# Softmax times V on one core: small tiles behind the large buffers, a flat spare loop, and loop code aligned to a fetch block

## The chip, the cores and the metric

The kernel runs on one core of a Trainium2 chip. The metric is the device time of one execution in microseconds; for a kernel's time the median of several executions is taken.

## The reference

```python
def reference(scores, v):          # scores [8, 12, 1024, 1024], v [8, 12, 1024, 64], float32
    scores_max = np.max(scores, axis=-1, keepdims=True)
    attn = np.exp(scores - scores_max)
    attn = attn / (np.sum(attn, axis=-1, keepdims=True) + 1e-8)
    return np.matmul(attn, v).astype(np.float32)
```

That is a softmax over the last axis of 96 given score matrices, each multiplied with its 1024 x 64 block of `v`. The scores are 403 MB, `v` and the output 25 MB each.

## The kernel before, in words

The 96 pairs of batch and head are called heads here. The main loop (`For_i` at L434) takes four heads an iteration (`AHEAD`), so it runs 24 times. It is of the kind "reg_based": the engines are not stopped between iterations, and semaphores only count upwards.

For each head, `heads` does the following. The scores of the head, 4 MB, have been loaded into one of four buffers `s_nat` (L218), with eight rows of the matrix in each of the 128 partitions. ScalarE takes `exp` of two rows per partition at a time without subtracting the maximum and writes float16 to `p_nat` (L386). TensorE transposes 128 x 128 blocks of that into PSUM (`psT`, L399); VectorE copies them to SBUF (`pt`, L406); TensorE multiplies them with `vones` (L165), which holds the head's `v` in float16 and a column of ones, so that the sum of each row comes out as column 64. VectorE takes the reciprocals of the sums into `seen` (L144) and scales the product into `out_sb` (L150). GpSimd copies the next `v` from `v_sb` into `vones` (L239). All loads and stores are issued by SyncE on one queue: `load_next` and `last` put the load of the head four further on behind the last use of the buffer, and the last iterations split the loads and stores into smaller ones.

Since the maximum is not subtracted and float16 is used, the kernel checks that this was allowed. `seen` collects the smallest and the largest reciprocal over the whole run, `v_seen` the range of `v` (L257). At the end of each iteration `judge` makes of these a count of partitions in which all was within bounds (`part`, `fits`, `right`, all tiles of 128 x 1 made by `small`) and leaves it in `count` (L274 to L298). Behind the loop every engine loads `count` into a register (L439) and compares it (L440):

```python
    good = nc.values_load(count[:], min_val=0, max_val=P)
    with tc.If(good < P, preferred_fallthrough_block=False):
        general()
```

`general()` is a plain float32 version with the maximum subtracted. With the data used here it is never run: each engine executes a few instructions of the other arm, jumps over the code of `general()` and goes on behind it to the closing barriers. In that arm SyncE, ScalarE, VectorE and TensorE bring the semaphores that `general()` would have raised to the values that they would have had.

`general()` has two nested loops: over the heads (one load of the scores, eight of `v`, one store) and inside it over the eight rows of a partition. The tiles `seen`, `v_seen`, `count` and those of `small` come from `const_pool`, which lies in SBUF ahead of `sb_pool` with the large buffers `s_nat`, `v_sb`, `p_nat`, `pt` and `out_sb`.

## Time and profile before

| | |
|---|---|
| median of three executions | 1073.61 us (1073.51 to 1074.58) |
| the profiled execution, its own time | 1074.27 us |
| its span, from the first to the last instruction | 1072.4 us |
| TensorE, weight loads, VectorE, ScalarE, GpSimd busy | 728.2, 694.7, 776.4, 740.4, 244.9 us |
| read from HBM, written | 436.21 MB, 25.17 MB |
| chain of work that ended last | DMA 60%, TensorE 10%, weight loads 6%, ScalarE 6%, VectorE 5% |

Busy times are summed over the span, so that none of the engines is busy for more than 72% of it. The DMA row of the 40 slices and the table of DMA queues count the 16 DMA engines of the core together. Names that end in q (SPq, DVEq) stand for the instructions that an engine's sequencer executes itself: branches, register moves, semaphores, DMA issues; the page does not count them as busy time. L12 is line 12 of the kernel.

### The profile page before, as it was taken

To read this page: it belongs to the slowest core of one execution; us is meant where nothing else is said; L and a number is where in the kernel's file an instruction comes from. 1 tells how busy PE (TensorE), PEld (TensorE's weight loads), DVE (VectorE), ACT (ScalarE), POOL (GpSimd) and SP (SyncE) were. 2 spreads that over 40 slices of the span, in tenths; PEclk is the share of its full clock that TensorE was granted. 3 is DMA by queue.
4 is the path that set the end of the run, shared out by engine and by line. 5 is a ranking of instruction groups with operands and counts; after the bars stand their busy time and mean duration, and the time that the engine had idled before them with its cause. 6 is when DMAs were issued, how large, how long until landed. Compare 5 with 4: busy or idle time off the path is not lost.

```text
span 1072.4 us, 33178 instructions
## 1 busy us (share of the span) xinstructions
PE 728.2 (68%) x12312; PEld 694.7 (65%) x12312; DVE 776.4 (72%) x1663; ACT 740.4 (69%) x480; POOL 244.9 (23%) x406
## 2 busy tenths in 40 slices
PE   2766766766766668676666766667767667667685
PEld 2665766666766667676666766666766667666574
DVE  1876776877767777777686776767767778677686
ACT  3766776766858667676666676766857667686684
POOL 3113112131121211221113112131121211222113
PEclk9887878878888788878887878878787788877888
DMA  9999999999999999999999999999999999999993
GB/s 395 433 417 431 428 439 431 430 425 438 433 433 431 429 433 423 438 430 430 430 429 432 430 433 431 430 431 432 426 441 431 433 430 429 432 423 438 430 423 139
DMA packets 25336, 453.09 MB, mean 423 GB/s; under 512 B 2800, under 2 KB 3312, under 8 KB 9712
## 3 DMA queue, kind: packets, MB, share of 16 engines
q1 hardware_dynamic: 25328, 453.00, 98.6%
q8 instruction: 4, 0.07, 0.0%
q14 instruction: 4, 0.03, 0.0%
HBM read 436.21 MB, written 25.17 MB: 430 GB/s over the span
## 4 chain that ended last, share of the span: by engine, by line
DMA 60%; PE 10%; PEld 6%; issue 6%; ACT 6%; DVE 5%; POOL 3%; SPq 1%; POOLq 1%; DVEq 0%; ACTq 0%; PEldq 0%
DMA s_nat<-in_scores_dram 60%; PE psT L399 6%; ACT p_nat L386 6%; PE psO L165 4%; PEld L399 4%; POOL vones L239 3%; PEld L165 2%; DVE pt L406 2%; DVE v_seen L257 1%; SPq L230 1%; SPq L218 0%; POOLq L239 0%; DVE v_seen L251 0%; DVE part L270 0%; POOLq L360 0%
## 5 line engine op out<-in xcount | busy, mean ns | idle before, releaser
L386 ACT ACTIVATE p_nat<-s_nat 128x2048 f16<-128x2048 f32 (+1 forms) x456 | 709.7, 1631 | 223.2 <-DMA s_nat<-in_scores_dram 176.6
L399 PE MATMUL psT<-order,p_nat 128*128 128x128 f16 x6144 | 571.0, 251 | 240.9 <-ACT p_nat L386 228.5
L406 DVE COPY pt<-psT 128x1024 f16<-128x1024 f16 x768 | 520.7, 687 | 221.8 <-PE psO L165 87.2
L399 PEld LDWEIGHTS <-p_nat 128*128 128x128 f16 x6144 | 462.1, 125 | 259.3 <-ACT p_nat L386 246.2
L239 POOL CAST vones<-v_sb 32x512 f16<-32x512 f32 x400 | 244.2, 610 | 819.3 <-PE L399 506.7
L165 PE MATMUL psO<-vones,pt 128*128 128x65 f16 x6144 | 360.0, 205 | 32.8 <-DVE v_seen L251 15.4
L165 PEld LDWEIGHTS <-pt 128*128 128x128 f16 x6144 | 301.9, 106 | 44.7 <-DVE pt L406 30.2
L150 DVE TENSOR_TENSOR out_sb<-psO,seen 64x256 f32<-64x256 f32 x384 | 161.9, 422 | 53.7 <-DMA out_dram<-out_sb 43.1
L386 ACT ACT_TABLE_LOAD x24 | 30.8, 1283 | 94.7 <-PE psO L165 49.9
L257 DVE TENSOR_REDUCE v_seen<-vones 128x1 f32<-128x512 f16 x96 | 65.6, 684 | 2.2
L294 PE MATMUL psO<-vones,right 128*1 128x1 f16 x24 | 3.9, 164 | 62.7 <-DVE right L278 62.7
L294 PEld LDWEIGHTS <-right 128*1 128x1 f16 x24 | 1.9, 79 | 65.7 <-DVE right L278 65.7
L144 DVE RECIPROCAL seen<-psO 128x4 f32<-128x4 f32 x192 | 33.8, 176 | 0.9 <-PE psO L165 0.2
L298 DVE CAST count<-psO 1x1 int32<-1x1 f32 x24 | 3.5, 146 | 6.1 <-PE psO L294 6.1
L274 DVE SCALAR_TENSOR_TENSOR part<-seen,fits 128x1 f32<-128x1 f32 x24 | 7.0, 291 | 0.8
L251 DVE TENSOR_REDUCE seen<-seen 128x1 f32<-128x33 f32 x24 | 4.5, 188 | 0.8
L278 DVE SCALAR_TENSOR_TENSOR right<-seen,part 128x1 f16<-128x1 f32 x24 | 4.2, 175 | 0.8
L252 DVE TENSOR_REDUCE seen<-seen 128x1 f32<-128x33 f32 x24 | 4.2, 176 | 0.0
L278 DVE SCALAR_TENSOR_TENSOR fits<-v_seen,part 128x1 f32<-128x1 f32 x24 | 3.6, 150 | 0.0
L252 DVE TENSOR_REDUCE v_seen<-v_seen 128x1 f32<-128x5 f32 x24 | 3.6, 148 | 0.0
L251 DVE TENSOR_REDUCE v_seen<-v_seen 128x1 f32<-128x5 f32 x24 | 3.5, 148 | 0.0
L270 DVE TENSOR_SCALAR part<-v_seen 128x1 f32<-128x1 f32 x24 | 3.5, 144 | 0.0
(10 smaller groups left out, 1.4 us busy)
## 6 DMA issues: line engine op xcount, KB each, us to landing
s_nat<-in_scores_dram SPq DMA_DIRECT2D x96, 4096.0 KB, 31.5
v_sb<-in_v_dram SPq DMA_DIRECT2D x24, 1024.0 KB, 18.8
out_dram<-out_sb SPq DMA_DIRECT2D x47, 512.0 KB, 26.3
s_nat<-in_scores_dram SPq DMA_DIRECT2D x2, 2048.0 KB, 32.3
s_nat<-in_scores_dram SPq DMA_DIRECT2D x1, 1536.0 KB, 32.6
s_nat<-in_scores_dram SPq DMA_DIRECT2D x3, 512.0 KB, 21.1
s_nat<-in_scores_dram SPq DMA_DIRECT2D x1, 1024.0 KB, 24.9
out_dram<-out_sb SPq DMA_DIRECT2D x1, 256.0 KB, 2.6
```

The source lines that it names most:

```text
L144: inverse = nc.vector.reciprocal(out=recip, in_=psO[:, :, D : D + 1])
L150: nc.vector.tensor_tensor(out=st["out_sb"][h * W : (h + 1) * W, t, b * G : (b + 1) * G, :], in0=psO[part, :, 0:D], in1=recip[part].to_broa ...
L165: product = nc.tensor.matmul(out=bank[:, g * M : (g + 1) * M], lhsT=pt[:, c * P : (c + 1) * P], rhs=st["vones"][:, c, 0:M], start=(c == 0) ...
L230: nc.sync.dma_start(out=v_sb[:].rearrange("x h s l d -> x (h s l d)"), in_=rows[bass.ds(n // AHEAD, 1)].rearrange("o x y -> (o x) y"),)
L239: spread = nc.gpsimd.tensor_copy(out=vones_bufs[k][s * Q : (s + 1) * Q, :, 0:D].rearrange("i (h l) d -> i h l d", l=L), in_=v_sb[k * Q : ( ...
L251: nc.vector.tensor_reduce(out=tile[:, 0:1], in_=tile[:, 0 : n + 1], axis=X, op=ALU.min)
L252: nc.vector.tensor_reduce(out=tile[:, n + 1 : n + 2], in_=tile[:, 1 : n + 2], axis=X, op=ALU.max)
L257: watch = nc.vector.tensor_reduce(out=v_seen[:, 1 + k : 2 + k], in_=vones_bufs[k][:, :, 0:D], axis=mybir.AxisListType.XY, op=ALU.max, appl ...
L278: nc.vector.scalar_tensor_tensor(out=out, in0=tile[:, 0:1], scalar=low, in1=part, op0=ALU.is_ge, op1=ALU.mult)
L386: exp = nc.scalar.activation(out=p_nat[:, g : g + rows, :].rearrange("p r (x v) -> p x r v", v=Q * L), in_=s_bufs[k][:, r + g : r + g + ro ...
L399: turned = nc.tensor.transpose(out=psT[:, c * P : (c + 1) * P], in_=p_row[:, c // L, c % L, :], identity=order16[:],)
L406: copy = nc.vector.tensor_copy(out=pt[:], in_=psT[:])
```

## The change

1. `seen`, `v_seen`, `count` and the tiles of `small` come from a new pool, `small_pool`, opened behind the large buffers. The large buffers thereby start at lower addresses, directly behind `vones`.
2. `general()` has one loop over 96 x 8 blocks of 128 rows in place of two nested ones, with three DMAs (one block of scores, the head's `v`, one block of the output), and uses `s_nat0` alone for its buffers.
3. The main loop names VectorE and SyncE in `head_align_engines`. For these two engines the loader puts the first instruction of an iteration at the start of a block of the size in which instructions are fetched; the padding in front of it is jumped over.

```diff
+    small_pool = ctx.enter_context(tc.tile_pool(name="small", bufs=1))
-    seen = const_pool.tile([P, 1 + AHEAD * R + 1], FP32, name="seen")
+    seen = small_pool.tile([P, 1 + AHEAD * R + 1], FP32, name="seen")
     nc.vector.memset(seen, 1.0)
-    v_seen = const_pool.tile([P, 1 + AHEAD + 1], FP32, name="v_seen")
+    v_seen = small_pool.tile([P, 1 + AHEAD + 1], FP32, name="v_seen")
     nc.vector.memset(v_seen, 1.0)
...
-        return const_pool.tile([P, 1], dtype, name=f"{name}{turn[name]}")
+        return small_pool.tile([P, 1], dtype, name=f"{name}{turn[name]}")
-    count = const_pool.tile([1, 1], I32, name="count")
+    count = small_pool.tile([1, 1], I32, name="count")
...
     def general():
-        s, x = s_bufs[0], s_bufs[1]
...
-        with tc.For_i(0, BH, 1) as n:
-            nc.sync.dma_start(out=s[:], in_=one(sc_bh, n))
-            for c in range(C):
-                nc.sync.dma_start(
-                    out=v1[:, c, 0:D],
-                    in_=v_n[bass.ds(n, 1)].rearrange("o p c d -> (o p) c d")[:, c, :],
+        s_rows = scores.rearrange("b h (r p) j -> (b h r) p j", p=P)
+        v_rows = v.rearrange("b h (c p) d -> (b h) p c d", p=P)
+        out_rows = out.rearrange("b h (r p) d -> (b h r) p d", p=P)
+        row, p_row, pt = (s_bufs[0][:, r, :] for r in range(3))
+        v1 = s_bufs[0][:, 3, 0 : C * M].rearrange("p (c m) -> p c m", m=M)
+        out_row = s_bufs[0][:, 4, 0:D]
...
+        with tc.For_i(0, BH * R, 1) as n:
+            nc.sync.dma_start(out=row, in_=s_rows[bass.ds(n, 1)].rearrange("o p j -> (o p) j"))
+            nc.sync.dma_start(
+                out=v1[:, :, 0:D], in_=v_rows[bass.ds(n // R, 1)].rearrange("o p c d -> (o p) c d")
+            )
...
-            with tc.For_i(0, R, 1) as r:
-                row = s[:, bass.ds(r, 1), :].rearrange("p o j -> p (o j)")
...
+            nc.vector.tensor_scalar(
+                out=out_row, in0=psO_bufs[2][:, 0:D], scalar1=den[:], scalar2=None, op0=ALU.mult
+            )
             nc.sync.dma_start(
-                out=out_n[bass.ds(n, 1)].rearrange("o p r d -> (o p) r d"), in_=out_bufs[0][:, 0]
+                out=out_rows[bass.ds(n, 1)].rearrange("o p d -> (o p) d"), in_=out_row
             )
...
-    with tc.For_i(0, BH, AHEAD, iteration_sync="reg_based") as n0:
+    aligned = [mybir.EngineType.DVE, mybir.EngineType.SP]
+    with tc.For_i(
+        0, BH, AHEAD, iteration_sync="reg_based", head_align_engines=aligned
+    ) as n0:
```

More of the change, by code (lines that the diff above doesn't have):

```diff
@@ L300, in general @@
     def general():
-        s, x = s_bufs[0], s_bufs[1]
-        out_n = out.rearrange("b h (p r) d -> (b h) p r d", p=P)
-        v_n = v.rearrange("b h (c p) d -> (b h) p c d", p=P)
+        s_rows = scores.rearrange("b h (r p) j -> (b h r) p j", p=P)
[3 more added lines that the diff above has]
+        v1 = s_bufs[0][:, 3, 0 : C * M].rearrange("p (c m) -> p c m", m=M)
@@ L305, in general @@
+        out_row = s_bufs[0][:, 4, 0:D]
         lift, den = small("lift"), small("den")
-        p_row, pt = x[:, 0, :], x[:, 1, :]
-        v1 = x[:, 2, 0 : C * M].rearrange("p (c m) -> p c m", m=M)
-        nc.vector.memset(x[:, 2, 0 : C * M], 1.0)
+        nc.vector.memset(s_bufs[0][:, 3, 0 : C * M], 1.0)
         half = SK // 2
-        with tc.For_i(0, BH, 1) as n:
-            nc.sync.dma_start(out=s[:], in_=one(sc_bh, n))
-            for c in range(C):
-                nc.sync.dma_start(
-                    out=v1[:, c, 0:D],
-                    in_=v_n[bass.ds(n, 1)].rearrange("o p c d -> (o p) c d")[:, c, :],
-                )
-            with tc.For_i(0, R, 1) as r:
-                row = s[:, bass.ds(r, 1), :].rearrange("p o j -> p (o j)")
-                nc.vector.tensor_reduce(out=lift, in_=row, axis=X, op=ALU.max, negate=True)
-                nc.scalar.activation(out=p_row, in_=row, func=EXP, bias=lift[:])
-                for c in range(C):
-                    at = c * P % half
-                    nc.tensor.transpose(
-                        out=psO_bufs[c * P // half][:, at : at + P],
-                        in_=p_row[:, c * P : (c + 1) * P],
-                        identity=ident32[:],
-                    )
-                for h in range(2):
-                    nc.vector.tensor_copy(out=pt[:, h * half : (h + 1) * half], in_=psO_bufs[h][:, 0:half])
-                for c in range(C):
-                    nc.tensor.matmul(
-                        out=psO_bufs[2][:, 0:M],
-                        lhsT=pt[:, c * P : (c + 1) * P],
-                        rhs=v1[:, c, :],
-                        start=(c == 0),
-                        stop=(c == C - 1),
-                    )
-                nc.vector.tensor_scalar(
-                    out=den, in0=psO_bufs[2][:, D : D + 1], scalar1=EPS, scalar2=None, op0=ALU.add
-                )
-                nc.vector.reciprocal(out=den, in_=den)
-                nc.vector.tensor_scalar(
-                    out=out_bufs[0][:, 0, bass.ds(r, 1), :].rearrange("p o d -> p (o d)"),
-                    in0=psO_bufs[2][:, 0:D], scalar1=den[:], scalar2=None, op0=ALU.mult,
-                )
@@ new lines, in general @@
+        with tc.For_i(0, BH * R, 1) as n:
[3 more added lines that the diff above has]
+            )
+            nc.vector.tensor_reduce(out=lift, in_=row, axis=X, op=ALU.max, negate=True)
+            nc.scalar.activation(out=p_row, in_=row, func=EXP, bias=lift[:])
+            for c in range(C):
+                at = c * P % half
+                nc.tensor.transpose(
+                    out=psO_bufs[c * P // half][:, at : at + P],
+                    in_=p_row[:, c * P : (c + 1) * P],
+                    identity=ident32[:],
+                )
+            for h in range(2):
+                nc.vector.tensor_copy(out=pt[:, h * half : (h + 1) * half], in_=psO_bufs[h][:, 0:half])
+            for c in range(C):
+                nc.tensor.matmul(
+                    out=psO_bufs[2][:, 0:M],
+                    lhsT=pt[:, c * P : (c + 1) * P],
+                    rhs=v1[:, c, :],
+                    start=(c == 0),
+                    stop=(c == C - 1),
+                )
+            nc.vector.tensor_scalar(
+                out=den, in0=psO_bufs[2][:, D : D + 1], scalar1=EPS, scalar2=None, op0=ALU.add
+            )
+            nc.vector.reciprocal(out=den, in_=den)
+            nc.vector.tensor_scalar(
+                out=out_row, in0=psO_bufs[2][:, 0:D], scalar1=den[:], scalar2=None, op0=ALU.mult
+            )
```

## The prediction

> **What bounds the kernel now.** I read the page first: the span, the 40 slices and the DMA queues.

> ```profile
> span 1072.4 us, 33178 instructions
> ...
> DMA  9999999999999999999999999999999999999993
> ...
> DMA packets 25336, 453.09 MB, mean 423 GB/s; under 512 B 2800, under 2 KB 3312, under 8 KB 9712
> ...
> q1 hardware_dynamic: 25328, 453.00, 98.6%
> ...
> q14 instruction: 4, 0.03, 0.0%
> ```

> The transfers of data alone keep the 16 DMA engines at work for 98.6% of the span, 0.986 x 1072.4 = 1057.4 us. No slice but the last falls under nine tenths. So the kernel is bound by its transfers until the last load has landed, and by something else in the last slice. To see the two apart I asked the DMA view for 0 to 1051 us, and then the table of windows for the end.

> ```profile
> DMA packets 24512, 451.59 MB, mean 430 GB/s; under 512 B 2713, under 2 KB 2713, under 8 KB 8899
> ...
> q1 hardware_dynamic: 24509, 451.55, 100.3%
> q8 instruction: 3, 0.05, 0.0%
> ...
> s_nat<-in_scores_dram SPq DMA_DIRECT2D x94, 4096.0 KB, 31.5
> ```

> ```profile
> 1010.00:1051.40 41.40, 30.27 (x536) 28.25 (x532) 32.89 (x71) 32.55 (x21) 10.19 (x17) 0.84 0.99 419
> 1051.40:1064.80 13.40, 8.50 (x156) 7.06 (x153) 12.65 (x34) 6.00 (x7) 4.86 (x8) 0.99 0.23 88
> 1064.80:1067.60 2.80, 0.00 (x0) 0.00 (x0) 0.00 (x0) 0.00 (x0) 0.04 (x1) 0.50 0.22 72
> 1067.60:1070.80 3.20, 0.00 (x0) 0.00 (x0) 0.00 (x0) 0.00 (x0) 0.00 (x0) 0.50 0.02 5
> 1070.80:1072.40 1.60, 0.00 (x0) 0.00 (x0) 0.00 (x0) 0.00 (x0) 0.00 (x0) 0.50 0.03 10
> ```

> The columns after the window's length are PE, PEld, DVE, ACT and POOL busy time, the granted clock, the DMA share and GB/s. Up to 1051.4 us the DMA engines are full. A load takes 31.5 us from issue to landing, and 4096 KB (4.194 MB) at 430 GB/s take 9.75 us, so some 22 us of other transfers are queued ahead of each load: a late issue, or a slow engine, is hidden as long as it costs less than that. After 1051.4 us nothing is queued ahead. There come 13.4 us of work on the last rows, 2.8 us that hold the last stores and a barrier, then 3.2 us in which no engine does anything and the DMA engines are 2% busy, and 1.6 us of closing barriers. The 3.2 us are the part to explain, so I asked for the lines of the skipped branch: L440 is the `If` behind the loop, L439 the value it tests, L467 the closing code.

> ```profile
> L440 SPq EVENT_SEMAPHORE  x8: 17/17/17, 1067.5 to 1068.0; - x8
> ...
> L440 SPq COMPARE_BRANCH  x2: 46/48/49, 1067.4 to 1068.0; - x2
> L440 ACTq COMPARE_BRANCH  x2: 46/48/49, 1067.4 to 1067.5; - x2
> ...
> L440 DVEq COMPARE_BRANCH  x2: 57/59/61, 1067.5 to 1067.7; - x2
> ```

> ```profile
> L439 SPq FUSED_REGOPS  x1: 181/181/181, 1070.8 to 1070.8; - x1
> L439 SPq SEQ_ASSERT  x1: 37/37/37, 1071.0 to 1071.0; - x1
> ```

> ```profile
> L467 POOLq DRAIN  x1: 39/39/39, 1067.6 to 1067.6; - x1
> L467 ACTq DRAIN  x1: 14/14/14, 1067.7 to 1067.7; - x1
> L467 PEldq DRAIN  x1: 8/8/8, 1068.0 to 1068.0; - x1
> L467 DVEq DRAIN  x1: 41/41/41, 1070.8 to 1070.8; - x1
> ```

> ```profile
> q14 instruction: 2, 0.02, 2.2%
> ```

> The second branch of L440 jumps over the code of `general()`. ScalarE jumps at 1067.5 and runs its next instruction (DRAIN) at 1067.7; GpSimd and TensorE are as quick. VectorE jumps at 1067.7 and SyncE at 1068.0, and both run nothing until 1070.8: 3.0 and 2.7 us, with nothing that they wait for. In just that window (1067.6 to 1070.7, last fence) there are two instruction transfers, 0.02 MB together, some 8 KB each. I read this as one fetch for each of the two engines: their target was not in the instruction memory. The other three had theirs. The two engines named in the change are the two that stall.

> **The change, part by part.** *Alignment of VectorE's and SyncE's loop code, and the flat loop.* By the program's listing there are 87 SyncE and 54 VectorE instructions between that jump and its target: two nested loops with their reset, skip and exit code, and ten DMAs. The flat loop has one set of this code and three DMAs, I count some 35 for each. With the loop's head at the start of a block, everything that runs to the end lies close behind it: VectorE has 135 instructions in an iteration and jumps at about the 142nd, to about the 176th; SyncE has 82 (and some 20 second words of DMAs), jumps at about the 106th, to about the 141st. The likeliest outcome is that both targets are held when the jump comes (what speaks against it for SyncE stands under the rivals). Then SyncE goes on after 0.2 us, as ScalarE does, and not after 2.7: 2.5 us off the path. It needs both engines: the closing barrier waits for all five. SyncE, the later one, sets the 2.5; VectorE's 3.0 fall beside it.

> *Fewer semaphores.* Where `general()` is skipped, SyncE makes up its DMAs' counts with eight EVENT_SEMAPHOREs, 1067.5 to 1068.0, 0.5 / 7 = 0.07 us each, ahead of its jump. Ten DMAs keep eight semaphores; three DMAs need three, so five go: 5 x 0.07 = 0.35 us. The closing waits shrink too:

> ```profile
> L467 SPq EVENT_SEMAPHORE  x10: 17/28/28, 1071.1 to 1072.3; - x10
> L467 SPq DRAIN  x3: 7/7/7, 1071.6 to 1071.9; - x3
> ```

> Eight of these ten stand between 1071.1 and the first DRAIN at 1071.6, 0.06 us each, each for two semaphores; with five semaphores fewer two go, 0.12 us. At the least both are worth nothing (if the allocator keeps eight), at the most 0.47 us. I take the whole, as the count follows from the DMAs.

> *The price of the alignment.* Padding ahead of the head makes the entry to the loop a jump into a block that nothing has touched, a stall like the one above, once for each engine.

> ```profile
> L434 SPq COMPARE_BRANCH  x25: 55/60/69, 17.7 to 1065.3; - x25
> ```

> ```profile
> L218 SPq EVENT_SEMAPHORE  x143: 17/28/7086, 18.5 to 1056.0; - x143
> ```

> ```profile
> L467 DVEq BRANCH_PREFETCH_HINT  x24: 39/39/56, 2.0 to 1029.5; - x24
> ```

> ```profile
> DVE pt L406 <- PE L399: 64.8, 111, 19.6
> ```

> SyncE enters at 17.7 us and from 18.5 waits 7.1 us for ScalarE before it can issue its next load. Behind SyncE's stall stand that load and all later issues; 2.7 us end inside the 7.1. While the DMA engines are full a fetch may take longer than the idle one at the end; past 7.1 us the load is issued late, and then the 22 us of queued transfers cover it. VectorE enters at 2.0 us and waits 19.6 us for its first transposes, so its 3.0 us end inside that. Both cost nothing. Without that cover each would cost its 2.7 or 3.0 us once. [...]

> Inside the loop there is nothing to gain: up to 1051 us the DMA view has no q14 transfer, so neither engine fetches there now.

> *The small tiles behind the large buffers.* Two memsets and the check's operations get other addresses; no instruction is added. The large buffers move down: 416 bytes of small tiles (seen, v_seen and eight more, each rounded up to 32) leave the space ahead of them, and by the allocator's list `s_nat0` goes from byte 21,920 (160 past a multiple of 256) to 21,504, an even multiple. No row shows such an offset changed, so I bound its cost. The DMA view gives, for 5 to 16 us (only 32 KB rows and 29 tiny packets that raise semaphores), 1063.5 to 1066 (512 stores of 1 KB, 48 tiny ones) and 1059.54 to 1059.66 (tiny ones alone):

> ```profile
> DMA packets 176, 4.82 MB, mean 438 GB/s; under 512 B 29, under 2 KB 29, under 8 KB 29
> ...
> q1 hardware_dynamic: 176, 4.82, 101.5%
> ```

> ```profile
> DMA packets 561, 0.54 MB, mean 216 GB/s; under 512 B 48, under 2 KB 560, under 8 KB 560
> ...
> q1 hardware_dynamic: 560, 0.52, 62.2%
> ```

> ```profile
> DMA packets 8, 0.00 MB, mean 0 GB/s; under 512 B 8, under 2 KB 8, under 8 KB 8
> ...
> q1 hardware_dynamic: 8, 0.00, 3.8%
> ```

> Tiny: 0.038 x 0.12 us x 16 engines / 8 = 9.1 ns each. 32 KB: (1.015 x 11 x 16 - 29 x 0.009) / 147 = 1213 ns. 1 KB: (0.622 x 2.5 x 16 - 48 x 0.009) / 512 = 47.7 ns. The last two differ by 31,744 bytes and 1166 ns, 36.7 ps a byte, so 1 KB of bytes is 37.6 ns and a packet's fixed part 10.1 ns. A tiny packet, which has no large buffer at either end, pays 9.1 of these already. What the offset can cost is the 1.0 ns that is left; by the page 25,328 - 2,800 = 22,528 packets carry data, which is 22,528 x 1.0 / 16 = 1.4 us at the most. A loss is bounded by no row; I set the same 1.4 us for that end. I take zero, as 1.0 ns is about the rounding of these shares.

> *Sum.* 2.5 + 0.47 = 3.0 us off a span of 1072.4, 1069.4. The profiled execution took 1074.27, 1.87 more than its span, so it would take 1071.3. The median of the three runs, 1073.61, is 0.66 below the profiled one; off that the sum gives 1070.6 us, 0.28% less. A measurement of this kernel can tell about 0.2% from no change, 2.15 us: the forecast is past that bound by 0.9 us only. Its own range is 1069.2 to 1071.6: 1.4 us for the offset below, the 0.47 missing and half the scatter of the runs above (1073.51 to 1074.58).

> **The rivals.** *SyncE still stalls.* A fetch is 8 KB, and the program's file holds 64 bytes an instruction, so that is 128 instructions. SyncE's loop and its jump (the 106th) fit into the first 128 behind the head, its target (the 141st) lies in the next. If those are not fetched ahead while the loop runs (each iteration begins with a prefetch hint for the back edge, and no q14 transfer ran ahead of need up to 1051 us), the jump misses as now. VectorE's gain is then worth nothing, and only the 0.47 us remain: 1073.1. For it: exactly this miss happens now. Against it, the DMA view from 1067.5 to 1072.4 in slices of 0.12 us:

> ```profile
> GB/s 0 0 0 0 0 0 0 0 0 67 0 67 0 0 0 0 0 0 0 0 0 0 0 0 0 0 0 0 0 0 0 0 67 67 0 0 0 0 0 0
> ```

> The first two transfers are the fetches for the jump; two more follow at 1071.4, after the engines go on. They look like the next block, fetched when one is entered; the jump into the padded head would bring the same.

> [...]

> *A fetch in the tail (slower).* VectorE's 135 instructions do not fit into one block of 128; the last seven, the check's, would begin the second. If that block is dropped in each iteration, VectorE stalls 3.0 us ahead of the check. In 23 iterations the queue covers it, in the last it stands on the path, between the last products and `count`; and SyncE's target, in its own second block, is as absent as now. That gives 1073.61 + 3.0 - 0.47 = 1076.1. It decides from the point where fewer blocks are held than the loop spans. Against it: VectorE's loop spans two such blocks today as well (135 are more than 128), without a fetch.

> **How the numbers follow.** The forecast gets 0.66: the stalls are plain, both engines are treated, and one jump each must land in a held block. SyncE still stalling gets 0.22, the offset 0.04, the fetch in the tail 0.08. Faster by over 0.2% are the offset (0.04) and nine tenths of the forecast (0.60): 0.64. Same are the rest of the forecast (0.06) and the rival without gain (0.22): 0.28. Slower: 0.08. The range runs from the forecast's lower end, 1069.2, through the rival without gain, 1073.1, with the scatter of the runs above it (0.8) to 1073.9; it leaves out 0.12.

> **What would show it.** Right: no 2.7 us gap between SyncE's L440 branch and L439's FUSED_REGOPS, none for VectorE, a span of 1069 to 1070, and three EVENT_SEMAPHOREs for eight; q14 transfers near 2 and 18 us instead of 1068; 430 GB/s up to 1051 as before. Wrong: the gap remains for SyncE; or the last load lands some 8 us earlier (the offset); or q14 transfers come in every iteration (the tail).

## The result, and the profile after

The changed kernel takes 1068.21 us (median of five executions, 1067.7 to 1069.19) against 1073.74 for the kernel before in the same comparison: ratio 0.9947, 95% interval 0.9933 to 0.9962. It is 5.5 us faster. The forecast of 1070.6 us had the sign right and about half of the size; 1068.21 lies below its range (1069.2 to 1073.9).

From the page of the changed kernel: the span, the DMA row of the 40 slices, the total of the DMA packets, and the queues of data and of instructions.

```profile
span 1067.4 us, 33173 instructions
...
DMA  9999999999999999999999999999999999999994
...
DMA packets 25337, 453.10 MB, mean 425 GB/s; under 512 B 2800, under 2 KB 3312, under 8 KB 9712
...
q1 hardware_dynamic: 25328, 453.00, 98.9%
...
q14 instruction: 5, 0.04, 0.0%
```

The same 25,328 data packets with the same 453.00 MB now need 0.989 x 1067.4 = 1055.7 us of the 16 engines and not 1057.4: the bound by the transfers has itself become shorter, which the prediction had put at zero. The lines of the skipped branch in the changed kernel (L440 is still the `If`, L439 the value that it tests):

```profile
L440 SPq EVENT_SEMAPHORE  x3: 17/17/17, 1065.0 to 1065.1; - x3
...
L440 SPq COMPARE_BRANCH  x2: 46/48/49, 1064.9 to 1065.2; - x2
...
L440 DVEq COMPARE_BRANCH  x2: 57/59/61, 1065.0 to 1065.2; - x2
```

```profile
L439 SPq FUSED_REGOPS  x1: 181/181/181, 1065.7 to 1065.7; - x1
...
L467 SPq EVENT_SEMAPHORE  x11: 17/28/28, 1064.3 to 1067.3; - x11
```

SyncE jumps at 1065.2 and goes on at 1065.7; the 2.7 us gap has become 0.5 us. Three semaphores are made up and not eight. So the stalls went and the semaphores with them, as the prediction said. To separate the tail from what lies ahead, take the moment at which VectorE writes `count`, the last thing that depends on data. The timeline's columns are start, duration, engine and instruction; first the kernel before, then the changed one.

```profile
1064.61 0.15 DVE L298 CAST count<-psO 1x1 int32<-1x1 f32 x1 [0.26 <-PE psO L294]
```

```profile
1062.16 0.15 DVE L299 CAST count<-psO 1x1 int32<-1x1 f32 x1 [0.26 <-PE psO L295]
```

Of the 5.0 us between the spans (1072.4 and 1067.4), 2.45 fall ahead of `count` and 2.58 behind it. The second half was forecast, the first was not. It shows in the DMA view from 1044 to 1060 us, in slices of 0.4 us (each digit is the mean busy share of the 16 engines in tenths): the kernel before, then the changed one.

```profile
DMA  9999999899999999973222220000000000059960
```

```profile
DMA  7998999999998523232000000039970000000000
```

Both rows go the same way: nines; then a few slices of two or three tenths, in which four (before) and five (changed) late engines of the 16 still carry loads; then zeros, less than a tenth; then the last big stores. The zeros begin at 1053.6 us before and at 1051.6 in the changed kernel, 2 us earlier. They last 11 slices before and 7 after, 4.4 and 2.8 us: in the first 8 and 4 of these the load has a single engine left, in the last three nothing moves. A load raises its semaphore 16 times, once for each engine as it ends, and the waiting engine goes on with the last of them: in the kernel before, one of the split final loads lands on its last engine at 1053.46 us, and ScalarE, idle for 1.0 us, goes on at 1053.55. When each engine raised the semaphore of the last of these loads, from the semaphore records of the trace:

| us | first | median | last but one | last | `count` |
|---|---|---|---|---|---|
| before | 1051.30 | 1051.74 | 1054.24 | 1057.22 | 1064.61 |
| changed kernel | 1049.48 | 1049.73 | 1052.04 | 1053.68 | 1062.16 |

Most engines finish 2 us earlier, the slowest one 3.5 us earlier. The lateness of the last engine is not an accident of the end. In the kernel before, three engines fall 1.6 us behind early, one after each of three 16 KB instruction fetches (queue q8, at 30.7, 44.0 and 52.6 us), and stay 2.4 to 2.6 us behind from 78 us on. A fourth falls behind evenly, by 1.16 us at 268 us, 2.44 at 520, 3.85 at 772 and 5.07 at 1020, some 4.9 us in 1000; it is the last one at the end.

Of the 3.5 us only 2.45 reach `count`. From the end of ScalarE's last `exp` to the start of VectorE's last copy into `pt` there are 2.25 us in the kernel before and 3.23 in the changed one, and VectorE is busy for 2.22 and 3.14 of them: it has about 1 us more work left there. x_small below is like the changed kernel in this (3.16 us), x_align and z_dve are like the kernel before (2.42 and 2.45).

### The profile page after: what moved, and what is told of

It reads as the page before. It is cut to its first block, busy times and chain, and to the rows that moved or that the text cites. A ratio compares the mean times of both kernels' runs of the same rounds, so it can differ in the third digit from the quotient of the medians.

```text
span 1067.4 us, 33173 instructions
## 1 busy us (share of the span) xinstructions
PE 731.8 (69%) x12312; PEld 699.8 (66%) x12312; DVE 776.4 (73%) x1663; ACT 740.3 (69%) x480; POOL 243.9 (23%) x406
## 2 busy tenths in 40 slices
DMA packets 25337, 453.10 MB, mean 425 GB/s; under 512 B 2800, under 2 KB 3312, under 8 KB 9712
## 3 DMA queue, kind: packets, MB, share of 16 engines
q1 hardware_dynamic: 25328, 453.00, 98.9%
## 4 chain that ended last, share of the span: by engine, by line
DMA 61%; PEld 10%; issue 7%; PE 6%; DVE 5%; ACT 4%; POOL 3%; SPq 1%; POOLq 1%; DVEq 0%; ACTq 0%; PEldq 0%
DMA s_nat<-in_scores_dram 61%; PEld L396 6%; ACT p_nat L383 4%; PEld L166 4%; POOL vones L240 3%; PE psO L166 3%; PE psT L396 3%; DVE pt L403 2%; DVE v_seen L258 1%; SPq L231 1%; SPq L219 0%; POOLq L240 0%; DVE fits L279 0%; DVE v_seen L252 0%; DVE part L271 0%
## 5 line engine op out<-in xcount | busy, mean ns | idle before, releaser
L166 PEld LDWEIGHTS <-pt 128*128 128x128 f16 x6144 | 305.6, 107 | 46.8 <-DVE pt L403 30.1
L295 PEld LDWEIGHTS <-right 128*1 128x1 f16 x24 | 1.9, 79 | 66.1 <-DVE right L279 66.1
## 6 DMA issues: line engine op xcount, KB each, us to landing
s_nat<-in_scores_dram SPq DMA_DIRECT2D x96, 4096.0 KB, 32.1
```

Source lines behind the costliest of these rows:

```text
L166: product = nc.tensor.matmul(out=bank[:, g * M : (g + 1) * M], lhsT=pt[:, c * P : (c + 1) * P], rhs=st["vones"][:, c, 0:M], start=(c == 0) ...
```

## The experiments

Three things needed telling apart: whether the 2.5 us ahead of `count` come from the addresses or from the loop code, what each of the three parts is worth alone, and what in the addresses matters. The second group below moves the buffers of one program and changes no instruction but one or two small memsets, so it tests the addresses with the instructions held constant. Ratios are to the kernel before, run on the same chip in the same comparison. Single profiles of kernels with the same loads differ by about 1 us in the place of `count` (1062.16 for the changed kernel, 1061.15 for its twin without the flat loop), so differences below that are not read from one.

### The parts alone

**x_small**, the small tiles alone.

```diff
-    seen = const_pool.tile([P, 1 + AHEAD * R + 1], FP32, name="seen")
+    seen = small_pool.tile([P, 1 + AHEAD * R + 1], FP32, name="seen")
...
-    count = const_pool.tile([1, 1], I32, name="count")
+    count = small_pool.tile([1, 1], I32, name="count")
```

> Only the small tiles move behind the large buffers; loop and general() as before. Theory A (the addresses shorten the transfers): the check's count is written 2.4 us earlier than before's 1064.6 us, the 2.7 us gap of SyncE behind L440 stays, 1073.7 - 2.5 = 1071.2 us. Rival B (the addresses do nothing, the 2.4 us ahead of the count come from the aligned loop code or by chance): 1073.7 us, count at 1064.6.

Measured: 1070.09 us, ratio 0.9958 (0.9944 to 0.9971), 4.1 us less. Its end, with the `If` at L441 here, still holds the stall:

```profile
L441 SPq COMPARE_BRANCH  x2: 46/48/49, 1063.0 to 1063.7; - x2
...
L440 SPq FUSED_REGOPS  x1: 181/181/181, 1066.6 to 1066.6; - x1
```

SyncE jumps at 1063.7 and runs on at 1066.6. So the largest part of the gain has nothing to do with instruction fetches. `count` is written at 1060.31, 4.3 us earlier than before (Theory A had expected 2.4). The DMA view, 1044 to 1060:

```profile
DMA  9999999999999632221000899200000000000029
```

The last load's landings: median 1049.89, last but one 1051.87, last 1051.91. The last engine, 3 us behind all others before (1057.22 against 1054.24), is now level with the next: only three zeros stand ahead of the stores.

**x_align**, the aligned loop code alone (the engines' names are shortened here).

```diff
-    with tc.For_i(0, BH, AHEAD, iteration_sync="reg_based") as n0:
+    with tc.For_i(0, BH, AHEAD, iteration_sync="reg_based",
+                  head_align_engines=[DVE, SP]) as n0:
```

> Only the loop heads of VectorE and SyncE are aligned; small tiles and the nested general() as before. Theory A: the targets of the jump come into held blocks by the alignment alone; both gaps go, the eight semaphores stay: 1073.7 - 2.2 = 1071.5 us, count at 1064.6. Rival B (the code has to be short as well: SyncE's target stands over 200 instructions behind the head): VectorE's gap goes, SyncE's 2.7 us stay, 1073.5 us. If instead the aligned code is what brings the count forward, the count comes at 1062.2 and the time is 1069 to 1071.

Measured: 1074.11 us, 0.9997 (0.9988 to 1.0006): nothing gained. Yet the stall is gone:

```profile
L440 SPq COMPARE_BRANCH  x2: 46/48/49, 1069.5 to 1070.2; - x2
...
L439 SPq FUSED_REGOPS  x1: 181/181/181, 1070.7 to 1070.7; - x1
```

What the tail gained had been lost ahead of it: `count` comes at 1066.79, 2.2 us later than before. In the DMA view of the end the zeros begin at 1053.6 as in the kernel before, but the single engine carries its load until 1058.8, and the stores have not begun when the view ends:

```profile
DMA  9999898999999999984333320000000000000000
```

The last load lands at 1051.89 in the median and at 1059.25 on the last engine, 2.0 us later than the 1057.22 of before, while the median is not even 0.2 us later. Engines lag from the beginning: at 17 us the last engine of a load is 2.0 us behind the median (0.15 in the kernel before), and at 27 us a second one has begun to lag (0.94 us, and about 1.5 in the next load). Just ahead of these come the instruction transfers that go with the aligned loop code, two of 8 KB at 7.6 and 13.3 us and two at 22.2 and 27.7. Which of the two laggards counts at the end is told by the last group of runs. The theory's 1071.5 us was missed for this reason, although both stalls went. The queues from 0 to 40 us, first in the kernel before, then in x_align (the fifth q14 transfer is one of 32 bytes):

```profile
q8 instruction: 1, 0.02, 0.2%
```

```profile
q14 instruction: 5, 0.03, 0.2%
q8 instruction: 1, 0.02, 0.2%
```

**x_flat**, the flat loop alone.

```diff
-        with tc.For_i(0, BH, 1) as n:
+        with tc.For_i(0, BH * R, 1) as n:
...
-            with tc.For_i(0, R, 1) as r:
```

> Only general() is flat; tiles and loop code as before. Theory A (a fetch block ends between the jump and its target, and a shorter jump still crosses it): both gaps stay, five semaphores of SyncE fewer, 1073.7 - 0.35 = 1073.4 us. Rival B (the shorter jump stays inside a held block): the gaps of VectorE, SyncE or both go; with both, 1073.7 - 2.5 = 1071.2 us.

Measured: 1074.08 us, 0.9998 (0.9988 to 1.0007). In the span the stall is gone here too, 0.2 us behind the jump; that it is because the shorter skipped code ends nearer to the loop is a guess that no run shows (the `If` is L436 in this kernel):

```profile
L436 SPq COMPARE_BRANCH  x2: 46/48/49, 1068.4 to 1068.7; - x2
...
L435 SPq FUSED_REGOPS  x1: 181/181/181, 1068.9 to 1068.9; - x1
```

The span is 1070.5 us, 1.9 shorter than before, but the profiled execution took 1075.0, that is 4.5 us more than its span where 1.8 to 1.9 are usual. The DMA view from 1060 to 1080 in slices of 0.5 us shows what comes behind the last instruction:

```profile
GB/s 0 0 0 0 0 0 0 0 0 104 352 316 275 2 0 0 0 0 0 33 0 0 0 0 16 0 0 0 0 16 0 0 0 0 0 0 0 0 0 0
...
q14 instruction: 2, 0.02, 0.3%
```

The two entries of 16 GB/s, at 1072.0 and 1074.5, are 8 KB each, the two q14 transfers. Instructions are still fetched twice after all recorded work, and that time counts in the kernel's. The stall left the span and not the execution.

**x_align_flat**, **x_small_align** and **x_small_flat**, the three pairs. They are made of the edits above, two at a time (shortened):

```diff
+    with tc.For_i(0, BH, AHEAD, ..., head_align_engines=[DVE, SP]) as n0:   # x_align_flat, x_small_align
+        with tc.For_i(0, BH * R, 1) as n:                                   # x_align_flat, x_small_flat
+    seen = small_pool.tile([P, 1 + AHEAD * R + 1], FP32, name="seen")       # x_small_align, x_small_flat
```

> Aligned loop heads and the flat general(); small tiles as before. Theory A: the tail's whole gain without that of the addresses: 1073.7 - 2.55 = 1071.2 us, count at 1064.6, packets of 32 KB at 1215 ns on average as before. Rival B (the code's place also brings the count forward): 1068.5 us.

> Small tiles behind, aligned loop heads, nested general(). Theory A (the four fetches of the two engines now run in the busy phase, at 7 to 28 us, and put one DMA engine 2 us behind for the rest of the kernel): gaps behind L440 under 0.6 us, the last loads land 4.2 us spread over the 16 DMA engines and not 2.35, count at 1062 and not 1060.3, 1068.2 + 0.35 = 1068.6 us. Rival B (the later count was chance): count at 1060.3, 1067.6 us.

> Small tiles behind, flat general(), loop code not aligned. Theory A (with the flat loop alone the instruction fetch is only moved behind the last instruction and still counts): no gap behind L440, 4.5 us around the span as with the flat loop alone, five semaphores fewer than with the small tiles alone, 1070.1 - 0.35 = 1069.7 us. Rival B (the stall is gone for good): 1070.1 - 2.5 = 1067.6 us.

| kernel | us | ratio (95%) | `count` | us around the span |
|---|---|---|---|---|
| x_align_flat | 1073.48 | 0.9991 (0.9982 to 1.0000) | 1066.98 | 1.8 |
| x_small_align | 1068.12 | 0.9944 (0.9930 to 0.9958) | 1061.15 | 1.8 |
| x_small_flat | 1069.95 | 0.9961 (0.9948 to 0.9975) | 1059.75 | 4.8 |

All that was forecast to bring the 3.0 us, without the small tiles, is worth 0.7 us, and its interval touches 1; both theories for x_align_flat (1071.2 and 1068.5 us) missed, as its `count` comes 2.4 us late as in x_align. The alignment with the small tiles is as fast as the whole change: beside these two the flat loop adds nothing that can be measured. The 1068.12 us and the `count` of x_small_align lie between its two theories and decide for neither. The flat loop with the small tiles has the earliest `count` of the six and pays 4.8 us around its span, close to what was expected (1069.7).

### What in the addresses matters

In the kernel before `s_nat0` begins 160 bytes past a multiple of 256, in the changed one on one. The durations of the packets between 90 and 1040 us, from the trace's packet records, are these means in ns:

| bytes past a multiple of 256 | 32 KB (scores) | 8 KB (`v`) | 4 KB (stores) |
|---|---|---|---|
| 160 (before) | 1214.98 | 312.9 | 159.9 |
| 0 (changed kernel) | 1213.05 | 309.0 | 159.2 |
| 32 (y_gap32) | 1216.1 | 314.4 | 159.9 |
| 64 (y_gap64) | 1215.1 | 313.3 | 159.9 |
| 128 (y_gap128) | 1214.8 | 312.0 | 159.9 |
| 256, that is 0 (y_gap256) | 1213.06 | 309.0 | 159.2 |
| scores 0, all others 32 (y_gap32_rest) | 1213.07 | 309.1 | 159.35 |
| scores 32, all others 0 (y_gap32_scores) | 1215.2 | 309.6 | 159.9 |

The excess is not spread evenly. With the buffers on a multiple of 256, 99% of the 32 KB packets take exactly 1213 ns. In the kernel before 45% take longer (1214, 1218 and 1221 most often), and they come in stretches. From 5 to 30 us none of 333 is longer; the first is at 31.7 us, behind the first instruction fetch of the span (q8, 30.7 us). From 48 to 64 us 189 of 209 are longer, from 68 to 76 us none of 100. It is not the mixture with loads of `v` and stores that does it: the first 8 KB packet behind the start comes at 43.7 us, the first store at 66.1, and from 48 to 64 us the 209 packets of scores share the engines only with 17 tiny ones that raise semaphores and one fetch:

```profile
DMA packets 227, 6.86 MB, mean 429 GB/s; under 512 B 17, under 2 KB 17, under 8 KB 17
...
q1 hardware_dynamic: 226, 6.85, 99.7%
q8 instruction: 1, 0.02, 0.4%
```

In the same stretch of x_small 17 of 207 are longer. x_align and x_flat, at the addresses of before, show its durations (1214.88 and 1214.95); x_small shows those of the changed kernel (1213.07). The sum over the packets of the kernel before: some 12,300 of 32 KB by 1.9 ns, 3,072 of 8 KB by 3.9 and 6,144 of 4 KB by 0.7 are about 40 us, 2.5 us for each of 16 engines. In the DMA view from 90 to 1040 us it is visible as bytes moved in the same time: before, then the changed kernel.

```profile
DMA packets 21952, 409.60 MB, mean 431 GB/s; under 512 B 2440, under 2 KB 2440, under 8 KB 8011
```

```profile
DMA packets 22043, 410.54 MB, mean 432 GB/s; under 512 B 2448, under 2 KB 2448, under 8 KB 8041
```

0.94 MB more at 432 GB/s are 2.2 us, which agrees with the 2 us by which the median engine ends earlier. The kernels of this group are the changed kernel with an unused tile, written once, ahead of the large buffers:

```diff
+    gap = sb_pool.tile([P, 8], FP32, name="gap")     # 32 bytes; 16, 32, 64 elements for 64, 128, 256 bytes
+    nc.vector.memset(gap, 0.0)
     s_bufs = ...
```

> The changed kernel with an unused tile of 32 bytes ahead of the large buffers, so that they start at 32 past a multiple of 256. Theory A (being off a multiple of 64 is what costs): packets of 32 KB 1215 ns on average, of 8 KB 313, one DMA engine falls behind by 5 us in 1000, 1068.2 + 4.5 = 1072.7 us. [...] Rival C (the other small-tile addresses, not the large buffers', matter): 1068.2 us.

> The same with an unused tile of 64 bytes: the large buffers start at 64 past a multiple of 256. Theory A (multiples of 64 are free): packets of 32 KB 1213 ns, of 8 KB 309, 1068.2 us. [...]

> The same with 128 bytes: half a grain of 256. Theory A (every start off a multiple of 256 costs, by one more piece of a transfer): half the packets longer, 32 KB 1214.5 to 1215.5 ns on average, 1072 to 1074 us. Rival B (128 is the grain and 64 was too small): 1213 ns, 1068.2 us.

> The changed kernel with an unused tile of 256 bytes ahead of the large buffers: they start at an odd multiple of 256 instead of a multiple of 1024. Theory A (256 is the grain): every packet of 32 KB 1213 ns, of 8 KB 309, 1068.2 us. Rival B (512 or 1024 is the grain): 32 KB at 1215 ns, 1073 us.

| kernel | bytes past 256 | us | ratio (95%) | last engine, final load |
|---|---|---|---|---|
| y_gap32 | 32 | 1074.98 | 1.0005 (0.9996 to 1.0014) | 1059.85 |
| y_gap64 | 64 | 1073.83 | 0.9996 (0.9987 to 1.0006) | 1059.34 |
| y_gap128 | 128 | 1073.30 | 0.9986 (0.9977 to 0.9995) | 1058.69 |
| y_gap256 | 0 | 1067.96 | 0.9938 (0.9925 to 0.9952) | 1052.81 |

Moved by 256 bytes the kernel keeps its whole gain; moved by 32, 64 or 128 it loses most or all of it. But for the size of one memset the instructions are the same in all four. So of the starts that were run only those on a multiple of 256 (0 and 256) keep the gain, multiples of 32, 64 and 128 alone do not, and the order of the tiles is not what counts. That the price is one more piece of a transfer, as Theory A for 128 bytes has it, no run shows. The price does not grow with the bytes past the boundary: 32 cost more than 128, and more than the 1072.7 us that were expected for them at the most.

Which buffers carry it: in **y_gap32_rest** the gap stands behind the score buffers (`s_nat` on a multiple of 256, `v_sb`, `p_nat`, `pt` and `out_sb` 32 past), in **y_gap32_scores** one gap of 32 stands ahead of them and one of 224 behind (only `s_nat` 32 past).

```diff
     s_bufs = ...
+    gap = sb_pool.tile([P, 8], FP32, name="gap")     # y_gap32_rest
...
+    gap = sb_pool.tile([P, 8], FP32, name="gap")     # y_gap32_scores
     s_bufs = ...
+    gap2 = sb_pool.tile([P, 56], FP32, name="gap2")  # y_gap32_scores
```

> The changed kernel with 32 unused bytes between the score buffers and v_sb: the scores stay on a multiple of 256, v_sb, p_nat, pt and out_sb are 32 past one. Theory A (each transfer pays for its own buffer's start): 32 KB at 1213 ns, 8 KB at 314, 4 KB at 159.9, under 1 us more than the changed kernel, 1068.2 to 1069.2 us. Rival B (it is the operands of the compute engines that matter): 1073 us or more.

> The other way round: the score buffers are 32 past a multiple of 256, v_sb and what follows on one again. Theory A: 32 KB at 1216 ns, 8 KB at 309; most of what 32 bytes ahead of all buffers cost, 1072.5 to 1074.5 us. Rival B (the scores do not matter): 1068.2 us.

Measured: y_gap32_rest 1069.41 us, 0.9953 (0.9940 to 0.9967), last engine 1054.36; y_gap32_scores 1073.49 us, 0.9992 (0.9983 to 1.0001), last engine 1058.74. The score buffers carry most of it; the others some 1 us (1069.41 against 1068.21, intervals that overlap). The times fit Theory A, the packets do not: the 8 KB loads into `v_sb`, 32 past, take 309.1 ns where 314 were expected, and the 4 KB stores out of `out_sb`, on a multiple of 256, take 159.9 as soon as the scores are off. So a transfer does not simply pay for the start of its own buffer.

### Which engine's alignment is worth its price

If the padding's fetches displace data, aligning only the engine that needs it should beat both kernels. **z_dve** and **z_sp** are the changed kernel with one engine named.

```diff
-    aligned = [mybir.EngineType.DVE, mybir.EngineType.SP]
+    aligned = [mybir.EngineType.DVE]     # z_dve;  [mybir.EngineType.SP] in z_sp
```

> The changed kernel with only VectorE's loop code aligned. Theory A (a stall in the tail is paid by the slower of the two engines, fetches in the busy phase push the last DMA engine back): SyncE's place is that of the flat loop alone, so it has no gap behind L440 in the span, but its fetch comes behind the last instruction and counts; two fetches at 7 to 14 us instead of four; 1069.5 us, between small tiles with flat loop (1069.95) and the changed kernel (1068.2). Rival B (VectorE's alignment carries the whole gain): 1068.2 us.

> The changed kernel with only SyncE's loop code aligned. Theory A: VectorE's fetch comes behind the last instruction and counts; two fetches at 22 to 28 us; 1069.5 us. Rival B (SyncE's alignment carries the whole gain): 1068.2 us. If neither z_dve nor z_sp gains over 1069.95, the stall counts in full as soon as one engine has it.

z_dve took **1066.35 us** (1065.88 to 1067.25), ratio 0.9928 (0.9915 to 0.9942): faster than the kernel before, and all of its runs lie below all of the changed kernel's (1067.7 to 1069.19), though the intervals of the two ratios overlap. z_sp took 1070.72, 0.9969 (0.9957 to 0.9981), with 4.6 us around its span as in x_flat. Both theories missed both kernels: z_dve is faster than either said, z_sp slower. In z_dve SyncE does not stall although it is not aligned:

```profile
L440 SPq COMPARE_BRANCH  x2: 46/48/49, 1062.3 to 1062.6; - x2
...
L439 SPq FUSED_REGOPS  x1: 181/181/181, 1062.8 to 1062.8; - x1
```

and its loads end together, at 1049.78 in the median, 1051.92 on the last but one and 1051.93 on the last engine, where the changed kernel's last engine needs until 1053.68. The low tail of its DMA row, 1044 to 1060, is the short one of x_small:

```profile
DMA  9899999999999433331000799400000000000997
```

With the flat loop SyncE runs on without alignment, 0.2 us behind its jump here and in x_flat. The late fetches of z_sp and x_flat (4.6 and 4.5 us around the span) are absent in z_dve (1.8 us), so they go with an unaligned VectorE. At 1020 us the last engine is behind the median by 2.14 us in z_dve, 1.97 in x_small and 2.32 in x_small_flat (no alignment), but by 3.60 in z_sp, 3.76 in the changed kernel, 2.94 in x_small_align and 2.74 in y_gap256: it is SyncE's alignment that makes the last engine later. VectorE's fetches set an engine back too (1.82 us at 17 us in z_dve), but at 1020 us five engines are 1.8 to 2.1 us late in z_dve, and four of them 1.7 to 2.0 in x_small, without any alignment: one more is hidden among them. Not all of the 1.9 us between z_dve and the changed kernel need come from the fetches: of the 2.5 us by which its `count` is earlier, 1.75 are the last landing and 0.8 the smaller rest of VectorE's work told of above, whose cause is open.

## Why the prediction was right or wrong

*The stalls in the tail.* Right, with its mechanism. From `count` to the end of the span the kernel before needs 7.8 us, the changed one 5.2: 2.6 less, where 2.5 + 0.35 + 0.12 = 3.0 was forecast. The 2.5 measured 2.2, since SyncE still spends 0.5 us behind its jump where ScalarE's 0.2 were assumed; the five semaphores were worth what was said; the closing waits did not shrink, so the 0.12 did not come. Where the fetches would come was right in kind: four q14 transfers come behind the two entries to the loop, at 7.5 to 27.6 us and not at 2 and 18, and a fifth at 1066.3, after SyncE has gone on.

*The price of the alignment.* **This step failed.** "Both cost nothing" was argued from engines that would wait anyhow, and that half holds. The rows of the loop branch and of the first instruction in the loop, in the changed kernel:

```profile
L432 DVEq COMPARE_BRANCH  x25: 63/69/81, 1.8 to 1062.3; - x25
L432 SPq COMPARE_BRANCH  x25: 55/60/69, 17.6 to 1062.9; - x25
```

```profile
L467 DVEq BRANCH_PREFETCH_HINT  x24: 39/39/56, 9.3 to 1026.7; - x24
L467 SPq BRANCH_PREFETCH_HINT  x24: 31/31/62, 23.7 to 1033.9; - x24
```

VectorE enters at 1.8 and runs at 9.3, SyncE at 17.6 and 23.7: 7.5 and 6.1 us, more than twice the 3.0 and 2.7 of idle DMA engines, and still inside the waits of 19.6 and 7.1 us that were named as cover. (A fetch of 8 KB itself takes 0.31 us; VectorE's first one starts at 7.5 us, 5.7 us after the jump, with the DMA engines full of data.) What was not priced is the fetch as a transfer. It is one packet (8 KB each at 7.5, 13.2, 22.1 and 27.6 us in the changed kernel) among DMA engines that are full, and the load ends with the slowest of the 16: the one that lands at 17.0 us has 15 engines within 0.12 us of its median and one 1.88 us behind it. At the addresses of before that gives back 2.2 us of `count` (x_align), all that the tail gains there. Without SyncE's alignment the change is 1.9 us better by the medians (z_dve), up to some 0.8 us of which may be VectorE's rest.

*The small tiles.* **This step failed, and it is the larger miss**: "I take zero", at the most 1.4 us; x_small measured 4.1. Two things were wrong. The 1.0 ns that bounded it came from 5 to 16 us, where even in the kernel before no packet is lengthened; over the whole run the mean excess is 1.9 ns, on packets that come in stretches, with score loads alone too. And a mean over engines was taken (divided by 16), where the slowest engine sets the end: the median engine gains 1.9 us in x_small, the last one 5.3. (A slip without weight: the 416 bytes are those of `seen`, `v_seen` and seven more tiles, 160 + 32 + 7 x 32, not eight.) The offset had 0.04 of the chance, with a last load some 8 us earlier. No run shows that term; what the runs showed in its place is a last landing 3.5 us earlier in the changed kernel and 5.3 in x_small. Each start that was run off a multiple of 256 made the packets longer (32, 64, 128 and 160 bytes past), and the price does not follow the bytes: packets of scores are 2 ns longer on the mean at 160 and 3 at 32.

*The sum.* The parts add up neither to the 3.0 of the forecast nor quite to the 5.5: 4.1 (x_small) and 0.7 (x_align_flat) make 4.8. The alignment is worth nothing alone (x_align) and 2.0 us beside the small tiles (x_small_align 1068.12, x_small 1070.09, measured in two comparisons; the intervals of their ratios overlap, the runs do not). That its fetches cost less where no engine lags by 5 us is argued from the landings and lies within their scatter of 1 us; no run shows it by itself.

*The other rivals.* SyncE does not stall: it runs on 0.5 us behind its jump in the changed kernel and x_align, 0.2 in x_flat and z_dve. That 8 KB are 128 instructions, on which two rivals rest, was taken from the program's file; no trace shows the size of an instruction. No fetch comes in each iteration: there are five q14 transfers in the whole span.

*What stays open.* Why one of the 16 engines falls behind at a steady rate, by 4.9 us in 1000 in the kernel before and by some 1.8 on the boundary; why the packets are longer in some stretches and not in others, and why stores are longer when only the scores are off; and why two fetches of 0.31 us each leave an engine 1.4 to 2.0 us behind. The packet records do not name their DMA engine. That SyncE's fetches fall on the engine that is late anyhow is therefore read from the landings with and without its alignment, and not from a run that put a fetch on another engine.

## What to carry to other kernels

In a kernel bound by its transfers, look at where the large buffers begin before looking at the tail: here a start off a multiple of 256 bytes cost 4 to 7 us of 1070, and moving a few hundred bytes of small tiles behind them took it back. Judge a load by its last engine, not by the mean share: in x_small the median engine gained 1.9 us and the last one 5.3, and in x_align the small transfers put among full queues cost 2.2 us of `count`, as much as the stalls that they replaced. And compare the span with the execution's time: in x_flat the stall left the span, 1.9 us shorter, and came back as 4.5 us around it where 1.8 to 1.9 are usual.
